# A decoder layer on one core: the last 128 tokens' post norm and residual by VectorE, with no part of it by GpSimd

## The chip, the cores and the metric

The kernel runs on one core of a Trainium2 chip. The metric is the device time of one execution, in microseconds (us); lower is better. The engines are called as in the profile: PE is TensorE's matmul and PEld its weight load, DVE is VectorE, ACT is ScalarE, POOL is GpSimd, SP is SyncE. A name with a q at its end (SPq, POOLq) is the queue of that engine, where DMAs are issued and semaphores are waited for.

## What is computed

One layer of a hybrid decoder trunk on 512 tokens of 1024 channels in float32. A half-step SwiGLU feed-forward network with 2816 hidden channels comes first, then a token mixer (a gated linear recurrence beside sliding-window attention), then a second half-step feed-forward network. Each sub-layer has an RMS norm on its input and another on its output ahead of the residual addition:

```python
def rms_norm(x, g):
    xf = x.astype(jnp.float32)
    y = xf * lax.rsqrt(jnp.mean(xf * xf, axis=-1, keepdims=True) + RMS_EPS)
    return (y * g.astype(jnp.float32)).astype(x.dtype)

def swiglu(x, w_gu, w_down):
    gate, up = jnp.split(x @ w_gu, 2, axis=-1)
    return (jax.nn.silu(gate) * up) @ w_down

x = x + 0.5 * rms_norm(swiglu(rms_norm(x, ffn1_pre_g[l]), ffn1_w_gu[l], ffn1_w_down[l]), ffn1_post_g[l])
...
x = x + rms_norm(y, mix_post_g[l])
x = x + 0.5 * rms_norm(swiglu(rms_norm(x, ffn2_pre_g[l]), ffn2_w_gu[l], ffn2_w_down[l]), ffn2_post_g[l])
```

The change concerns the very last line, and of it the last 128 tokens: the norm of the second network's output `y`, its gain `ffn2_post_g`, and the addition of `x`.

## The kernel before

Nearly all the time goes into matmuls, and float32 products are made of three matmuls each: both operands are split into a high part (rounded) and a low part (the rest), and high times high, high times low and low times high are summed in PSUM. Up to the end, the activations lie transposed, with channels over the 128 partitions and tokens along the free dimension. The kernel goes through the first network, the mixer and the second network in that order. ScalarE rounds the weights to their high parts and VectorE makes the low parts, some steps ahead of the matmuls that use them. The order of the instructions on each engine is the order in which the program writes them; each engine works through its own in order, and waits on semaphores for the others.

The end of the second network makes the output with tokens over the partitions, so that a row of the output can be stored as it is. It goes through the tokens in four blocks of 128, `tb` from 0 to 3. For each block, `ybl` banks in PSUM collect the last hidden channels' part of the down projection (`mm3_out`, lines 1532 to 1534), and the parts of earlier hidden channels lie summed up in the SBUF tiles `yp_b` (in the code `parts[tb, dh]`, with `dh` the left or right 512 output channels). The last block is cut into three pieces, `pieces`: piece 0 is the left 512 columns, piece 1 the next 256, piece 2 the last 256. The earlier blocks have two pieces of 512. Between pieces 0 and 1 of the last block, TensorE transposes the residual `xT` into two PSUM banks, `otp` (in the code `tp`, line 1635).

When the matmuls of a piece are finished:

- line 1642: VectorE adds the PSUM bank to `yp_b`, or subtracts `yp_b` from it (the right half was summed with the other sign).
- line 1643: ScalarE squares the piece, with the sum over the columns going to a column of `ss` by an accumulator that is read at the end.
- line 1649: GpSimd multiplies the piece by the gain, `grow`, in place. It has to wait for the square, which reads the same columns. In the last block's piece 2 it is VectorE (line 1647) that does this, and it writes to another tile, `last`, so that it needn't wait for the square.

When all pieces of a block are through, VectorE adds up the sums of squares (lines 1645 and 1651 for the last block, 1653 for the others), ScalarE takes the root (line 1656), VectorE the reciprocal (line 1657), which gives the scale `rs` of each token. Then VectorE multiplies each piece by `rs` and adds the residual from `otp` in one operation (line 1665), and SyncE issues the store of the piece (line 1666). The last block's piece 1 goes another way: ScalarE has copied the residual's columns from PSUM to the SBUF tile `tail` beforehand (line 1638), scales the piece by `rs` (line 1662), GpSimd adds `tail` (line 1663), and ScalarE's queue issues the store.

After the last instruction, the program closes on line 1691: SyncE waits for all stores, each engine drains, and all report to GpSimd.

Of the kernel before, what the change touches and what calls it, by code (L numbers as in the profile page):

```python
# [11 lines left out]
AF = mybir.ActivationFunctionType  # L12
ALU = mybir.AluOpType
# [3 lines left out]
T = 512  # L17
# [99 lines left out]
def tile_layer(ctx: ExitStack, tc: tile.TileContext, out: bass.AP, **ins: bass.AP):  # L117
    nc = tc.nc
    pe, dve, act, pool, sync = nc.tensor, nc.vector, nc.scalar, nc.gpsimd, nc.sync
# [15 lines left out]
    def bank(name):  # L135
        return psum.tile([P, T], F32, tag="bank", name=name)

    def t2k(name, dt=F32):
        return big.tile([P, T], dt, tag="t2k", name=name, bufs=NT2K)

    def wt(name, w=T, dt=F32):
        return tmp.tile([P, w], dt, tag="w", name=name, bufs=NW)
# [1139 lines left out]
    scale = HD ** -0.5  # L1282
# [210 lines left out]
    for c in range(EARLY):  # L1493
# [9 lines left out]
        if c == EARLY - 2:  # L1503
            bcs = [l.spread() for l in lrms]
            for ci in range(KC):
                for h in range(2):
                    dve.tensor_mul(hl[ci][:, HALF[h]], hl[ci][:, HALF[h]], bcs[h])
                y = t2k(f"ylh{ci}", F32R), t2k(f"yll{ci}", F32R)
# [20 lines left out]
    def mm3_out(ps, h, tb, w, k, cs, start, stop):  # L1529
        (hh, hl_), (hi, lo) = h, w  # L1530
        blk = slice(tb * P, (tb + 1) * P)
        pe.matmul(ps, hh[:, blk], hi[:, k, cs], start=start, stop=False)  # L1532
        pe.matmul(ps, hh[:, blk], lo[:, k, cs], start=False, stop=False)  # L1533
        pe.matmul(ps, hl_[:, blk], hi[:, k, cs], start=False, stop=stop)  # L1534
# [69 lines left out]
    grow = [t2k(f"grow{dh}") for dh in range(2)]  # L1604
# [6 lines left out]
    def weights(f, dh):  # L1611
        k = f - f % 2, dh
        if k not in wd:
            assert order[len(wd)] == k
            wd[k] = W.take(min(3, len(order) - 1 - len(wd)))
        return wd[k]

    for tb in range(NB):
        end = tb == NB - 1
        pieces = [(0, 0, T)] + ([(1, 0, T // 2), (1, T // 2, T)] if end else [(1, 0, T)])  # L1620
        banks = [bank(f"ybl{tb}{i}") for i in range(len(pieces))]
        steps = [(i, f) for i in range(len(pieces)) for f in range(f0, f1)]
        if tb == 0:
            steps = [(i, f) for fs in (range(f0, f0 + 4), range(f0 + 4, f1)) for i in range(2) for f in fs]
        ss = small.tile([P, 3], F32, tag="ss3", name=f"ss_b{tb}")
        tot = small.tile([P, 1], F32, tag="tot", name=f"tot_b{tb}")
        for i, f in steps:
            dh, c0, c1 = pieces[i]
            if (i, f) == (1, f1 - 1 if tb == 0 else f0):

                tp = []
                for h in range(2):
                    tp.append(bank(f"otp{tb}{h}"))
                    for c in range(4):
                        pe.transpose(tp[h][:, c * P:(c + 1) * P], xT[4 * h + c][:, tb * P:(tb + 1) * P], ident)
                if end:
                    tail = wt("tail")[:, :T // 2]
                    act.copy(tail, tp[1][:, :T // 2])
            mm3_out(banks[i][:, :c1 - c0], hs[f - f0], tb, weights(f, dh), f % 2, slice(c0, c1), f == f0, f == f1 - 1)
            if f == f1 - 1:  # L1640
                y = parts[tb, dh][:, c0:c1]
                (dve.tensor_sub if dh else dve.tensor_add)(y, banks[i][:, :c1 - c0], y)  # L1642
                act.activation(wt(f"ysq{tb}{i}")[:, :c1 - c0], y, AF.Square, accum_out=ss[:, i:i + 1])  # L1643
                if end and i == 2:
                    dve.tensor_add(tot, ss[:, 0:1], ss[:, 1:2])
                    last = wt("last")[:, :c1 - c0]
                    dve.tensor_mul(last, y, grow[dh][:, c0:c1])
                else:
                    pool.tensor_mul(y, y, grow[dh][:, c0:c1])  # L1649
        if end:  # L1650
            dve.tensor_add(tot, tot, ss[:, 2:3])
        else:
            dve.tensor_add(tot, ss[:, 0:1], ss[:, 1:2])

        rs = small.tile([P, 1], F32, tag="rs1", name=f"rs_b{tb}")
        act.activation(rs, tot, AF.Sqrt, bias=eps4, scale=4.0 / D)
        dve.reciprocal(rs, rs)
        for i, (dh, c0, c1) in enumerate(pieces):
            y = parts[tb, dh][:, c0:c1]
            if end and i == 1:  # L1660

                act.activation(y, y, AF.Copy, scale=rs)
                pool.tensor_add(y, y, tail)
            else:
                dve.scalar_tensor_tensor(y, last if end and i == 2 else y, rs, tp[dh][:, c0:c1], op0=ALU.mult, op1=ALU.add)
            (act if end and i == 1 else sync).dma_start(out[0, tb * P:(tb + 1) * P, dh * T + c0:dh * T + c1], y)


# [26 lines left out]
```

## Time and profile before

| what | value |
|---|---|
| time, median of 3 runs | 879.47 us (879.43 to 879.74) |
| time of the profiled execution | 880.96 us |
| span of the profiled execution | 879.2 us |
| granted TensorE clock, mean | 0.994 |
| PE busy | 866.2 us (99%), 5732 instructions |
| DVE busy | 680.0 us (77%), 982 instructions |
| ACT busy | 491.3 us (56%), 839 instructions |
| POOL busy | 176.0 us (20%), 179 instructions |

The span runs from the first instruction to the last of one execution that the profiler recorded; its own time is 1.8 us longer than its span and 1.5 us longer than the median of the runs that were timed without a profile. Busy times are sums over the whole span and say little about the last ten microseconds, where TensorE has nothing left to do.

### The profile page before, as it was taken

To read this page: it belongs to the slowest core of one execution; us is meant where nothing else is said; L and a number is where in the kernel's file an instruction comes from. 1 tells how busy PE (TensorE), PEld (TensorE's weight loads), DVE (VectorE), ACT (ScalarE), POOL (GpSimd) and SP (SyncE) were. 2 spreads that over 40 slices of the span, in tenths; PEclk is the share of its full clock that TensorE was granted. 3 is DMA by queue.
4 is the path that set the end of the run, shared out by engine and by line. 5 is a ranking of instruction groups with operands and counts; after the bars stand their busy time and mean duration, and the time that the engine had idled before them with its cause. 6 is when DMAs were issued, how large, how long until landed. Compare 5 with 4: busy or idle time off the path is not lost.

```text
span 879.2 us, 14431 instructions
## 1 busy us (share of the span) xinstructions
PE 866.2 (99%) x5732; PEld 795.2 (90%) x5732; DVE 680.0 (77%) x982; ACT 491.3 (56%) x839; POOL 176.0 (20%) x179
## 2 busy tenths in 40 slices
PE   9999999999999999999999999999999999999995
PEld 8988999989989998998787899888998998998995
DVE  4979758768678864889999589678788789888744
ACT  6647534544435554466787456445556657567542
POOL 2010000000000014444465055211102303205213
PEclk9999999999999999999999999999999999999998
DMA  7242343242243243321311140226573947839901
GB/s 241 74 148 84 103 127 114 73 133 84 73 143 97 84 148 116 97 84 62 109 36 48 49 144 2 96 74 201 188 255 104 229 125 166 196 97 243 279 26 73
DMA packets 91556, 106.10 MB, mean 121 GB/s; under 512 B 4752, under 2 KB 76768, under 8 KB 90976
## 3 DMA queue, kind: packets, MB, share of 16 engines
q1 hardware_dynamic: 83408, 85.64, 30.8%
q0 software_dynamic: 7936, 19.41, 9.5%
q8 instruction: 45, 0.74, 0.3%
q14 instruction: 23, 0.19, 0.1%
q10 hardware_dynamic: 144, 0.13, 0.0%
HBM read 87.86 MB, written 17.30 MB: 120 GB/s over the span
## 4 chain that ended last, share of the span: by engine, by line
PE 91%; DVE 5%; ACT 1%; issue 1%; DMA 1%; POOL 0%; SPq 0%; POOLq 0%; DVEq 0%; ACTq 0%
PE aa L772 12%; PE ab L772 10%; PE da L772 6%; PE db L772 5%; PE ya L408 4%; PE ya L406 4%; PE ya L407 4%; PE ba L772 3%; PE bb L772 3%; PE a_first L948 2%; PE yb L1533 1%; PE yb L1532 1%; PE yb L1534 1%; PE ya L1549 1%; PE ya L1550 1%; PE ya L1551 1%
## 5 line engine op out<-in xcount | busy, mean ns | idle before, releaser
L1558 POOL DMA_DIRECT2D yp_b<-stage x42 | 36.5, 1146 | 147.2 <-ACT stage L1556 138.1
L406 PE MATMUL ya<-hha,whi_ad 128*128 128x512 f32 x158 | 61.5, 389 | 0.0
L407 PE MATMUL ya<-hla,whi_ad 128*128 128x512 f32 x158 | 61.5, 389 | 0.0
L408 PE MATMUL ya<-hha,wlo_ad 128*128 128x512 f32 x158 | 61.5, 389 | 0.0
L1049 POOL MEMSET bd_w_rg<- 128x512 f32 x1 | 0.5, 527 | 266.0 <-PE aa L772 266.0
L408 PEld LDWEIGHTS ya<-hha,wlo_ad 128*128 128x128 f32 x158 | 29.7, 188 | 6.2
L407 PEld LDWEIGHTS ya<-hla,whi_ad 128*128 128x128 f32 x158 | 29.7, 188 | 6.1
L406 PEld LDWEIGHTS ya<-hha,whi_ad 128*128 128x128 f32 x158 | 29.7, 188 | 6.0
L1107 DVE TENSOR_TENSOR yp_a<-ya,yp_a 128x512 f32<-128x512 f32 x24 | 16.4, 686 | 8.8 <-PE ya L408 8.8
L1532 PE MATMUL yb<-whi_bd,hhb 128*128 128x512 f32 x48 | 18.7, 389 | 0.0
L1533 PE MATMUL yb<-wlo_bd,hhb 128*128 128x512 f32 x48 | 18.7, 389 | 0.0
L1534 PE MATMUL yb<-whi_bd,hlb 128*128 128x512 f32 x48 | 18.7, 389 | 0.0
L578 POOL TENSOR_TENSOR acca_r<-acca_r,sq_r 128x512 f32<-128x512 f32 x6 | 8.4, 1406 | 48.1 <-ACT sq_r L437 48.1
L183 DVE TENSOR_TENSOR wlo_bd<-raw_bd,whi_bd 128x1024 fp32r<-128x1024 f32 x10 | 12.1, 1222 | 7.0 <-ACT whi_bd L178 7.0
L1649 POOL TENSOR_TENSOR yp_b<-yp_b,grow 128x512 f32<-128x512 f32 (+1 forms) x8 | 9.7, 1219 | 32.7 <-ACT ysq L1643 32.7
L425 PE MATMUL an<-xh_mx,whi_xl 128*128 128x256 f32 x64 | 15.9, 289 | 0.0
L426 PE MATMUL an<-xh_mx,wlo_xl 128*128 128x256 f32 x64 | 15.5, 283 | 0.0
L705 POOL TENSOR_TENSOR usb<-usb,gsb 128x512 f32<-128x512 f32 x5 | 7.6, 1537 | 33.0 <-DVE usb L702 21.8
L406 PE MATMUL gt<-xh_mx,whi_gt 128*128 128x512 f32 x32 | 14.2, 443 | 0.0
L1643 ACT ACTIVATE ysq<-yp_b 128x512 f32<-128x512 f32 (+1 forms) x9 | 5.2, 583 | 15.1 <-DVE yp_b L1642 14.6
L1532 PE MATMUL ybl<-whi_bd,hhb 128*128 128x512 f32 (+1 forms) x36 | 13.5, 375 | 0.0
L1533 PE MATMUL ybl<-wlo_bd,hhb 128*128 128x512 f32 (+1 forms) x36 | 13.2, 366 | 0.0
(1726 smaller groups left out, 3654.8 us busy)
## 6 DMA issues: line engine op xcount, KB each, us to landing
yp_b<-stage POOLq DMA_DIRECT2D x50, 256.0 KB, 8.2
raw_bd<-in_ffn_w_down SPq DMA_DIRECT2D x4, 1024.0 KB, 8.0
xn<-in_x SPq DMA_DIRECT2D x8, 256.0 KB, 5.2
raw_q<-in_w_in SPq DMA_DIRECT2D x4, 512.0 KB, 3.7
xT_hbm<-xT POOLq DMA_DIRECT2D x2, 1024.0 KB, 11.4
yp_b<-yp_b POOLq DMA_DIRECT2D x8, 256.0 KB, 4.3
xT<-xT_hbm POOLq DMA_DIRECT2D x2, 1024.0 KB, 8.1
out_dram<-yp_b SPq DMA_DIRECT2D x7, 256.0 KB, 2.9
```

What stands on the lines that cost most here:

```text
L406: pe.matmul(ps, hi[:, k, :], xh, start=start, stop=False)
L407: pe.matmul(ps, hi[:, k, :], xl, start=False, stop=False)
L408: pe.matmul(ps, lo[:, k, :], xh, start=False, stop=stop)
L425: pe.matmul(ps[:, sl], hi[:, k, :], xh, start=k == 0, stop=False)
L426: pe.matmul(ps[:, sl], lo[:, k, :], xh, start=False, stop=False)
L772: pe.matmul(o, w[:, k, js], x, start=first and i + j + k == 0, stop=k == 3 and i == 2, skip_group_check=True)
L948: pe.matmul(banks[j][:, HALF[0]], ws[j][part][:, k, :], n1.xs[k][xpart][:, HALF[0]], start=k == 0 and part == xpart, stop=stop and k == KD ...
L1107: dve.tensor_add(parts[c], b, parts[c])
L1532: pe.matmul(ps, hh[:, blk], hi[:, k, cs], start=start, stop=False)
L1533: pe.matmul(ps, hh[:, blk], lo[:, k, cs], start=False, stop=False)
L1534: pe.matmul(ps, hl_[:, blk], hi[:, k, cs], start=False, stop=stop)
L1558: pool.dma_start(parts[2 * tb + i, dh], st, accum_op=ALU.add)
```

## The change

In the last block, all multiplications by the gain are done by VectorE in place, the copy `tail` and the tile `last` are gone, and piece 1 is scaled and added by the same VectorE operation as the other two, with the residual read from PSUM. Its store stays on ScalarE's queue. The first three blocks are as they were. In the built program, the last block's VectorE instructions stand in this order: subtraction or addition of piece 0, multiplication of piece 0, subtraction of piece 1, multiplication of piece 1, subtraction of piece 2, sum of two squares, multiplication of piece 2, sum with the third, reciprocal, and three scalings with addition. GpSimd's last operation is the multiplication of the third block's right half. TensorE's instructions are the same, and so are all that stand before this block on the other engines.

```diff
@@ -1633,9 +1633,6 @@
                     tp.append(bank(f"otp{tb}{h}"))
                     for c in range(4):
                         pe.transpose(tp[h][:, c * P:(c + 1) * P], xT[4 * h + c][:, tb * P:(tb + 1) * P], ident)
-                if end:
-                    tail = wt("tail")[:, :T // 2]
-                    act.copy(tail, tp[1][:, :T // 2])
             mm3_out(banks[i][:, :c1 - c0], hs[f - f0], tb, weights(f, dh), f % 2, slice(c0, c1), f == f0, f == f1 - 1)
             if f == f1 - 1:
                 y = parts[tb, dh][:, c0:c1]
@@ -1643,10 +1640,7 @@
                 act.activation(wt(f"ysq{tb}{i}")[:, :c1 - c0], y, AF.Square, accum_out=ss[:, i:i + 1])
                 if end and i == 2:
                     dve.tensor_add(tot, ss[:, 0:1], ss[:, 1:2])
-                    last = wt("last")[:, :c1 - c0]
-                    dve.tensor_mul(last, y, grow[dh][:, c0:c1])
-                else:
-                    pool.tensor_mul(y, y, grow[dh][:, c0:c1])
+                (dve if end else pool).tensor_mul(y, y, grow[dh][:, c0:c1])
         if end:
             dve.tensor_add(tot, tot, ss[:, 2:3])
         else:
@@ -1657,12 +1651,7 @@
         dve.reciprocal(rs, rs)
         for i, (dh, c0, c1) in enumerate(pieces):
             y = parts[tb, dh][:, c0:c1]
-            if end and i == 1:
-
-                act.activation(y, y, AF.Copy, scale=rs)
-                pool.tensor_add(y, y, tail)
-            else:
-                dve.scalar_tensor_tensor(y, last if end and i == 2 else y, rs, tp[dh][:, c0:c1], op0=ALU.mult, op1=ALU.add)
+            dve.scalar_tensor_tensor(y, y, rs, tp[dh][:, c0:c1], op0=ALU.mult, op1=ALU.add)
             (act if end and i == 1 else sync).dma_start(out[0, tb * P:(tb + 1) * P, dh * T + c0:dh * T + c1], y)
```

## The prediction, as it was made ahead of the run

> **What bounds the kernel now.** I read the page first, then the chain that ended last over the final 15 us, then the timeline of each engine there, then the closing instructions (line 1691).
>
> ```profile
> span 879.2 us, 14431 instructions
> PE 91%; DVE 5%; ACT 1%; issue 1%; DMA 1%; POOL 0%; SPq 0%; POOLq 0%; DVEq 0%; ACTq 0%
> ```
>
> TensorE holds 91% of the chain, and the change touches none of its instructions. Only what follows TensorE's last matmul can move.
>
> ```profile
> 869.74 0.28 PE L1534 MATMUL ybl<-whi_bd,hlb 128*128 128x256 f32 x1
> ```
>
> TensorE is done at 870.02, so 9.2 us of the 879.2 are the tail. The end of the chain (start, length, what):
>
> ```profile
> 865.17 1.29 POOL yp_b L1649
> ...
> 868.75 1.98 POOL yp_b L1649 x2
> 870.74 1.71 issue
> 872.44 0.76 POOLq L1691
> ```
>
> The chain ends in GpSimd's queue, on line 1691, which is where the program closes: each engine drains, reports, and GpSimd collects the reports. The chain follows it only to 873.2, when GpSimd's last addition is done. The closing instructions that start before 878 (count, shortest/median/longest in ns, first and last start) show the rest:
>
> ```profile
> L1691 SPq EVENT_SEMAPHORE  x9: 28/28/28, 873.5 to 875.5; - x9
> L1691 SPq DRAIN  x2: 7/7/7, 875.6 to 875.7; - x2
> L1691 PEldq DRAIN  x1: 2345/2345/2345, 867.7 to 867.7; - x1
> L1691 DVEq DRAIN  x1: 1122/1122/1122, 872.0 to 872.0; - x1
> L1691 POOLq DRAIN  x1: 5991/5991/5991, 872.4 to 872.4; - x1
> L1691 ACTq DRAIN  x1: 148/148/148, 873.6 to 873.6; - x1
> ```
>
> SyncE waits for the stores one after another and is through at 875.7. TensorE's drain ends at 870.1, VectorE's at 873.1, ScalarE's at 873.8. GpSimd's begins at 872.44 and lasts 5.99 us, to 878.43. Only then does GpSimd take its first semaphore:
>
> ```profile
> L1691 POOLq EVENT_SEMAPHORE  x4: 17/17/17, 878.5 to 879.1; - x4
> ```
>
> So the last arrival is GpSimd's drain and not the stores: 2.8 us pass between SyncE's 875.7 and GpSimd's 878.5, and the closing takes the remaining 0.7 us to 879.2. That is the wait to argue about. The work that feeds it, VectorE, then ScalarE, GpSimd and SyncE (start, length, line, operation, idle time before it):
>
> ```profile
> 867.24 0.68 DVE L1642 TENSOR_TENSOR yp_b<-ybl,yp_b 128x512 f32<-128x512 f32 x1
> 868.62 0.42 DVE L1642 TENSOR_TENSOR yp_b<-ybl,yp_b 128x256 f32<-128x256 f32 x1 [0.70 <-PE ybl L1534]
> 870.06 0.42 DVE L1642 TENSOR_TENSOR yp_b<-ybl,yp_b 128x256 f32<-128x256 f32 x1 [1.01 <-PE ybl L1534]
> 870.40 0.35 DVE L1645 TENSOR_TENSOR tot_b<-ss_b 128x1 f32<-128x1 f32 x1
> 870.67 0.41 DVE L1647 TENSOR_TENSOR last<-yp_b,grow 128x256 f32<-128x256 f32 x1
> 871.12 0.16 DVE L1651 TENSOR_TENSOR tot_b<-tot_b,ss_b 128x1 f32<-128x1 f32 x1
> 871.90 0.75 DVE L1665 SCALAR_TENSOR_TENSOR yp_b<-yp_b,rs_b,otp 128x512 f32<-128x512 f32 x1
> 872.57 0.47 DVE L1665 SCALAR_TENSOR_TENSOR yp_b<-last,rs_b,otp 128x256 f32<-128x256 f32 x1
> ```
>
> ```profile
> 867.96 0.63 ACT L1643 ACTIVATE ysq<-yp_b 128x512 f32<-128x512 f32 x1 [2.34 <-DVE yp_b L1642]
> 868.49 0.18 ACT L1643 ACTIVATION_READ_ACCUMULATOR ysq<-yp_b 128x1 f32 x1
> 868.59 0.35 ACT L1638 COPY tail<-otp 128x256 f32<-128x256 f32 x1
> 869.42 0.42 ACT L1643 ACTIVATE ysq<-yp_b 128x256 f32<-128x256 f32 x1 [0.48 <-ACT tail L1638]
> 869.75 0.19 ACT L1643 ACTIVATION_READ_ACCUMULATOR ysq<-yp_b 128x1 f32 x1
> 870.57 0.42 ACT L1643 ACTIVATE ysq<-yp_b 128x256 f32<-128x256 f32 x1 [0.64 <-DVE yp_b L1642]
> 870.90 0.19 ACT L1643 ACTIVATION_READ_ACCUMULATOR ysq<-yp_b 128x1 f32 x1
> 871.89 0.51 ACT L1662 ACTIVATE yp_b<-yp_b,rs_b 128x256 f32<-128x256 f32 x1 [0.29 <-DVE rs_b L1657]
> 873.24 0.37 ACTq L1666 DMA_DIRECT2D out_dram<-yp_b  x1
> ```
>
> ```profile
> 872.48 0.73 POOL L1663 TENSOR_TENSOR yp_b<-yp_b,tail 128x256 f32<-128x256 f32 x1 [1.74 <-ACT yp_b L1662]
> ```
>
> ```profile
> 872.68 0.81 SPq L1666 DMA_DIRECT2D out_dram<-yp_b  x2
> ```
>
> **The change, part by part.** *Removed from GpSimd:* its last three operations, two multiplications (1.98 us) and the closing addition (0.73 us). Its last operation becomes the multiplication of the block before, 865.17 to 866.46, so its drain is reached 7.3 us sooner. Two bounds for when it ends then: with the lag that VectorE's drain has behind VectorE's last operation (873.10 against 873.04) it is 866.5; with the lag that GpSimd's has now (878.43 against 873.21, 5.2 us) it is 871.7. Either way it is hidden by the stores, by 4 us or more, so which one holds does not matter. The 2.8 us go. What is late next is SyncE's report that the stores have landed.
>
> *Added to VectorE:* three multiplications written in place, where one wrote to another tile, and one scaling-and-addition of 256 columns. An in-place multiplication must wait until ScalarE has squared the same columns, and VectorE runs in order, so behind each waiting multiplication stands the subtraction that feeds ScalarE's next square. An operation on 512 columns with both operands in SBUF takes 684 ns, by this row:
>
> ```profile
> L785 DVE TENSOR_TENSOR g1b<-g1b,u4b 128x512 f32<-128x512 f32 x8 | 5.5, 684 | 0.3 <-ACT g1b L806 0.3
> ```
>
> One of 256 takes 0.41 (line 1647). An operation with nothing to wait for starts 0.08 before its forerunner ends (872.57 against 872.65), and one that waits for ScalarE starts 0.03 after it (871.12 against 871.09). Step by step:
>
> 1. Piece 0's square is read at 868.67, as now. Its multiplication runs from 868.70 to 869.38.
> 2. Piece 1's subtraction starts at 869.30 instead of 868.62 and ends at 869.72.
> 3. Piece 1's square follows 0.09 later, as piece 2's does now (870.48 to 870.57), at 869.81: the copy that delays it now (0.48 idle, by its row) is gone. Square and read take 0.52, to 870.33.
> 4. Piece 1's multiplication runs from 870.36 to 870.77; piece 2's subtraction starts at 870.69 instead of 870.06. TensorE has long finished.
> 5. Piece 2's square starts 0.51 after the subtraction does and takes 0.52, to 871.72. Its multiplication starts at 871.75, and the sum of the squares at 872.08 instead of 871.12: 0.96 later.
> 6. From that sum to the first scaling-and-addition it is 0.78, as now: 872.86. The second starts 0.67 later, at 873.53, the third 0.39 later, at 873.92, and ends at 874.39.
> 7. The stores: piece 0 at 873.64 instead of 872.68 (+0.96); piece 1 from ScalarE's queue at 874.03; piece 2 from SyncE's at 874.42, last, where piece 1's at 873.24 is last now (+1.18).
>
> *Removed from ScalarE:* the copy (0.35 us) and the scaling (0.51 us); step 3 uses the one, and the other leaves the path with the addition. ScalarE's queue then holds only its store, which waits for VectorE.
>
> *The stores* are the same three, 256, 128 and 128 KB on the same queues. If moving the 512 KB limits, the landing shifts with the first issue, by 0.96; if the last issue limits, by 1.18. I take 1.1, nearer to the last issue, since the issues now spread over 0.8 us instead of 0.56.
>
> **The sum.** 2.8 us of waiting for the drain go, and 1.1 us come on the store path: -1.7 us, between -1.84 and -1.62. The profiled execution took 880.96 us, 1.8 over its span, and 1.5 over the median of the runs; I expect the same distances, so it becomes 879.3 with a span of 877.5. On the median, 879.47 - 1.7 = 877.8 us.
>
> The short sum of squares on line 1645 took 0.35 us while GpSimd was multiplying (to 870.73), the same operation on line 1651 took 0.16 with GpSimd idle. That 0.19 goes, but the sum then lies under the square of step 5, so by these rows it is worth nothing. The Trainium skill, "Perfetto Trace Analysis", section "Optimizing Scalar/DVE Operations", says that GpSimd and VectorE share a read port to SBUF, so that moving work between the two may bring nothing. The trace agrees that they hinder each other; by the rule, GpSimd's multiplications cost VectorE time already and the move would cost up to those 0.19 us less than step 7 has, a sum of -1.9.
>
> **Rivals.** *The drain is not GpSimd's own work* (slower). Its 5.99 us could wait on what the whole tail does, or be long only in a profiled execution. The place is the same drain. If its end keeps its distance to the last store's issue (878.43 against 873.24), it moves by 1.18 to 879.6. If it isn't there in a timed run, both kernels end with their stores and the store path's 1.1 is all that is left. Either way +1.2, 880.7; it decides as soon as the new drain ends after about 876.8. For it: the other engines' drains end within 0.2 us of their last work, GpSimd's 5.2 us after, and nothing in the trace says why. Against it: no other engine's work lies between 873.8 and 875.4, so an engine that waited for the others would have had nothing to wait for beyond 875.7. A longer ScalarE lag in steps 3 and 5 could carry it past +1.76. I give it 17%. The Trainium skill, "VectorE: DVE Perf Modes", section "The DRAIN you can't avoid", says that the drains before and after a kernel are a constant of about 12 ns on all five engines: by that rule GpSimd's drain would be no price of GpSimd's work, which is this rival. The trace disagrees for this drain, with its 5991 ns.
>
> *A store lands late.* The earlier stores of 256 KB took longer from issue to landing than the last ones:
>
> ```profile
> out_dram<-yp_b SPq DMA_DIRECT2D x7, 256.0 KB, 2.9
> ```
>
> The last store now needs 2.2 us (873.24 to the semaphores that SyncE takes up to 875.5). At 2.9 it adds 0.7: -1.0, 878.5 us. Against: none of the three last stores did so. 9%.
>
> *The change does not do what it says* is excluded: in the built order GpSimd's last operation is the multiplication of the block before, and VectorE's tail has the operations of steps 1 to 6 in that order.
>
> **How the numbers follow.** A measurement of this kernel can tell about 0.2%, 1.76 us, from no change. The forecast (74%) lies at -1.7, just inside; with 0.2 us of error in the steps it falls on either side of that line, so 35% go to faster and 39% to the same. The slower rival gives 10% to the same and 7% to slower, the late store 9% to the same. Faster 0.35, same 0.58, slower 0.07. The forecast's own range is 877.2 to 878.3; to keep 8 in 10 with the two rivals, it reaches up to 880.7.
>
> **What would show it.** Right: GpSimd's drain starts near 865.2 and ends before SyncE's last wait; the chain ends with a store's landing, with no idle time before GpSimd's first closing semaphore other than SyncE's; the sum of squares starts near 872.1 and VectorE ends near 874.4. Wrong: GpSimd's drain still ends last, or the last store is issued before 874 or after 874.8.

## The result, and the profile after

The changed kernel takes 877.46 us, the median of 10 runs (876.76 to 877.91). The kernel before, run beside it, takes 879.55 us (10 runs, 878.92 to 881.13). The ratio is 0.9974, with a 95% interval of 0.9964 to 0.9984: 2.1 us less, clear of no change, and beyond the prediction's line of 0.2% by its middle but not by the whole of the interval. The profiled execution took 877.85 us. Of the experiments below, one of e2's 11 runs took 2223 us, with TensorE slow throughout, and the times of e4 lie in two groups some 2 us apart, so e2 is read from the profile of e5, the same kernel once more, and e4 from its tail.

```profile
span 876.1 us, 14426 instructions
```

The span is 3.1 us shorter than before's 879.2, but 1.05 us of that has nothing to do with the change, as TensorE's last matmul shows (start, length):

```profile
868.69 0.28 PE L1534 MATMUL ybl<-whi_bd,hlb 128*128 128x256 f32 x1
```

It ends at 868.97, against 870.02 before, although TensorE's instructions are the same, and in e1 below, which has the whole change in it, it ends at 870.02 again. The granted clock was 0.998 in this execution and 0.994 in that of before; that this alone makes the 1.05 is not shown. So the two kernels are compared by their tails, from the end of the last matmul to the end of the span: 9.2 us before, 7.15 after, 2.05 less, which is what the timed runs say too. To compare a moment of this trace with one of before, add 1.05. The closing, now on line 1680, without its last 0.7 us (count, shortest/median/longest in ns, first and last start):

```profile
L1680 SPq EVENT_SEMAPHORE  x10: 17/28/28, 873.7 to 875.2; - x10
L1680 SPq DRAIN  x2: 7/10/13, 875.3 to 875.4; - x2
L1680 POOLq DRAIN  x1: 6556/6556/6556, 864.1 to 864.1; - x1
L1680 PEldq DRAIN  x1: 2345/2345/2345, 866.7 to 866.7; - x1
L1680 DVEq DRAIN  x1: 1570/1570/1570, 871.8 to 871.8; - x1
L1680 ACTq DRAIN  x1: 147/147/147, 873.3 to 873.3; - x1
L1680 POOLq EVENT_SEMAPHORE  x1: 17/17/17, 875.4 to 875.4; - x1
```

GpSimd's drain now starts at 864.09 and ends 6.56 us later, at 870.64. That is 4.7 us before SyncE is through with the stores, at 875.37, and GpSimd takes its first semaphore at once, at 875.39. The 2.8 us between SyncE and GpSimd are gone. The drain itself did not get shorter. GpSimd's last operation is now the one ahead of the last block:

```profile
864.12 1.29 POOL L1643 TENSOR_TENSOR yp_b<-yp_b,grow 128x512 f32<-128x512 f32 x1 [1.40 <-ACT ysq L1640]
```

It ends at 865.42, and the drain ends 5.23 us behind it. Before, the last operation ended at 873.21 and the drain at 878.43, also 5.23 us behind. This lag is what the experiments follow. VectorE's tail, then ScalarE's (start, length, line, operation, idle time before it):

```profile
867.67 0.69 DVE L1643 TENSOR_TENSOR yp_b<-yp_b,grow 128x512 f32<-128x512 f32 x1 [0.79 <-ACT ysq L1640]
868.27 0.42 DVE L1639 TENSOR_TENSOR yp_b<-ybl,yp_b 128x256 f32<-128x256 f32 x1
869.32 0.42 DVE L1643 TENSOR_TENSOR yp_b<-yp_b,grow 128x256 f32<-128x256 f32 x1 [0.62 <-ACT ysq L1640]
869.66 0.42 DVE L1639 TENSOR_TENSOR yp_b<-ybl,yp_b 128x256 f32<-128x256 f32 x1
869.99 0.15 DVE L1642 TENSOR_TENSOR tot_b<-ss_b 128x1 f32<-128x1 f32 x1
870.71 0.43 DVE L1643 TENSOR_TENSOR yp_b<-yp_b,grow 128x256 f32<-128x256 f32 x1 [0.57 <-ACT ysq L1640]
871.05 0.15 DVE L1645 TENSOR_TENSOR tot_b<-tot_b,ss_b 128x1 f32<-128x1 f32 x1
871.76 1.53 DVE L1654 SCALAR_TENSOR_TENSOR yp_b<-yp_b,rs_b,otp 128x512 f32<-128x512 f32 x3
```

```profile
868.77 0.42 ACT L1640 ACTIVATE ysq<-yp_b 128x256 f32<-128x256 f32 x1 [1.14 <-issue]
870.17 0.42 ACT L1640 ACTIVATE ysq<-yp_b 128x256 f32<-128x256 f32 x1 [0.89 <-DVE tot_b L1642]
872.94 0.37 ACTq L1655 DMA_DIRECT2D out_dram<-yp_b  x1
```

Each multiplication waits for ScalarE's square of the same columns (0.79, 0.62 and 0.57 us idle), and the subtraction of the next piece stands behind it. The chain that ended last now runs through this tail. The view follows it only to VectorE's last operation; the landing of the stores and SyncE's waits come after it. Before, it ended in GpSimd's queue:

```profile
871.76 0.75 DVE yp_b L1654
872.51 0.39 DVEq L1680
872.90 0.39 DVE yp_b L1654
```

### The profile page after: what moved, and what is told of

Same layout as the page of the kernel before. It is cut to its first block, busy times and chain, and to the rows that moved or that the text cites. A ratio compares the mean times of both kernels' runs of the same rounds, so it can differ in the third digit from the quotient of the medians.

```text
span 876.1 us, 14426 instructions
## 1 busy us (share of the span) xinstructions
PE 864.9 (99%) x5732; PEld 793.9 (91%) x5732; DVE 681.5 (78%) x985; ACT 490.5 (56%) x837; POOL 172.9 (20%) x176
## 5 line engine op out<-in xcount | busy, mean ns | idle before, releaser
L1643 POOL TENSOR_TENSOR yp_b<-yp_b,grow 128x512 f32<-128x512 f32 x6 | 7.7, 1288 | 30.4 <-ACT ysq L1640 30.4
```

## The experiments

**The theory and its rival.** The theory is the prediction's: the drain follows GpSimd's own last operation by a fixed lag, so the program ends with the drain or with the stores, whichever is later. The rival is that the end of the drain follows what the whole tail does, or the stores, and that it came earlier in the changed kernel for another reason than GpSimd's own last operation. The layer's kernels are compared by the tail and by the lag:

| kernel | last matmul ends | GpSimd's last operation ends | drain ends | lag | SyncE through | span ends | tail |
|---|---|---|---|---|---|---|---|
| before | 870.02 | 873.21 | 878.43 | 5.23 | 875.68 | 879.23 | 9.2 |
| after | 868.97 | 865.42 | 870.64 | 5.23 | 875.37 | 876.14 | 7.15 |
| e1 | 870.02 | 873.05 | 878.28 | 5.23 | 876.41 | 879.07 | 9.06 |
| e5 | 868.21 | 872.61 | 877.84 | 5.23 | 875.07 | 878.63 | 10.42 |
| e3 | 868.67 | 865.12 | 870.34 | 5.23 | 874.09 | 874.86 | 6.19 |
| e4 | 870.40 | 871.12 | 876.34 | 5.23 | 875.87 | 877.14 | 6.74 |
| g3 | 868.23 | 871.41 | 875.98 | 4.57 | 873.89 | 876.77 | 8.54 |
| g4 | 868.14 | 864.59 | 869.82 | 5.23 | 874.54 | 875.31 | 7.16 |

**e1: one tiny operation on GpSimd, late.** The changed kernel, and a 128x1 product that nobody reads:

```diff
         dve.reciprocal(rs, rs)
+        if end:
+            z = small.tile([P, 1], F32, tag="z", name="z")
+            pool.tensor_mul(z, rs, rs)
```

> The changed kernel, with one GpSimd multiplication of 128x1 added after the reciprocal, whose result nobody reads. The tail (from the end of TensorE's last matmul to the end of the span) is 9.2 us before the change and 7.1 after it. Theory (GpSimd's drain ends 5.2 us after GpSimd's last operation, whatever its size): the operation ends about 3.0 us into the tail, the drain at 8.2, the tail is 8.9 to 9.0, and the time is 1.8 us above the changed kernel's, about 879.3. Rival (the drain grows with the work that GpSimd did, or waits on the other engines): the tail stays at 7.1 to 7.3 and the time at 877.5.

Measured: 879.59 us, median of 11 runs; the ratio to before is 1.0004 (0.9995 to 1.0013).

```profile
872.86 0.19 POOL L1654 TENSOR_TENSOR z<-rs_b 128x1 f32<-128x1 f32 x1 [6.39 <-DVE rs_b L1651]
L1683 POOLq DRAIN  x1: 5457/5457/5457, 872.8 to 872.8; - x1
L1683 SPq DRAIN  x2: 7/7/7, 876.3 to 876.4; - x2
```

One operation of 0.19 us gives the whole gain back. The drain ends at 878.28, 1.9 us after SyncE is through. VectorE, ScalarE and the stores are those of the changed kernel (SyncE is through 6.39 us after the last matmul, there 6.40), so it is GpSimd's own last operation, however small, that sets the drain.

**e2 and e5: the in-place multiplications alone.** The kernel before, with the three multiplications by VectorE in place; the copy, ScalarE's scaling and GpSimd's closing addition stay:

```diff
-                    last = wt("last")[:, :c1 - c0]
-                    dve.tensor_mul(last, y, grow[dh][:, c0:c1])
-                else:
-                    pool.tensor_mul(y, y, grow[dh][:, c0:c1])
+                (dve if end else pool).tensor_mul(y, y, grow[dh][:, c0:c1])
...
-                dve.scalar_tensor_tensor(y, last if end and i == 2 else y, rs, tp[dh][:, c0:c1], op0=ALU.mult, op1=ALU.add)
+                dve.scalar_tensor_tensor(y, y, rs, tp[dh][:, c0:c1], op0=ALU.mult, op1=ALU.add)
```

> The kernel before, with the three multiplications of the last block by VectorE in place, as the change has them; the copy, ScalarE's scaling and GpSimd's closing addition stay. Theory (the end is GpSimd's last operation plus 5.2 us plus 0.7, and VectorE's waits for the squares put that operation off by 0.96): the tail grows from 9.2 to 10.2 us and the time by 1.0, to 880.5. Rival (the drain's end does not follow GpSimd's last operation): the stores have 2.8 us of room, so the tail stays at 9.2 and the time at 879.5.

Measured: 880.82 us, median of 11 runs, ratio 1.0015 (1.0006 to 1.0024). The profile is that of e5, the same kernel once more:

> The same kernel as in e2 (the kernel before with the in-place multiplications by VectorE), once more, for a profile that can be laid beside the others. Theory (GpSimd's closing addition 0.96 us later, drain 5.2 us after it): the addition ends 4.1 to 4.2 us after TensorE's last matmul, where it is 3.2 before the change, and the tail is 10.1 to 10.2 us. Rival (the drain does not follow the addition): tail 9.2 us.

Measured: 880.36 us in one run (before beside it 879.87), and a tail of 10.42 us.

```profile
867.93 0.28 PE L1534 MATMUL ybl<-whi_bd,hlb 128*128 128x256 f32 x1
871.89 0.72 POOL L1660 TENSOR_TENSOR yp_b<-yp_b,tail 128x256 f32<-128x256 f32 x1 [7.23 <-ACT yp_b L1659]
L1688 POOLq DRAIN  x1: 5984/5984/5984, 871.9 to 871.9; - x1
```

GpSimd's addition ends 4.40 us after the last matmul, against 3.19 before, and the drain moves with it, 1.2 us. That is 0.2 to 0.3 us more than was expected, for the addition and for the tail. The copy on line 1638 is still there, and with it ScalarE starts the square of piece 1 0.37 us after the subtraction ends (868.31 against 867.94), where it is 0.08 in the changed kernel, which has no copy (868.77 against 868.69). Two of GpSimd's three tail operations are gone here, and nothing is gained. By itself that part of the change is a loss: it is GpSimd's last operation that counts, and the in-place multiplications on VectorE make that one later.

**e3: the waits of the in-place multiplications.** The changed kernel, with the products in tiles of their own, so that they needn't wait for the squares:

```diff
-                (dve if end else pool).tensor_mul(y, y, grow[dh][:, c0:c1])
+                if end:
+                    yg.append(wt(f"yg{i}")[:, :c1 - c0])
+                    dve.tensor_mul(yg[i], y, grow[dh][:, c0:c1])
+                else:
+                    pool.tensor_mul(y, y, grow[dh][:, c0:c1])
...
-            dve.scalar_tensor_tensor(y, y, rs, tp[dh][:, c0:c1], op0=ALU.mult, op1=ALU.add)
+            dve.scalar_tensor_tensor(y, yg[i] if end else y, rs, tp[dh][:, c0:c1], op0=ALU.mult, op1=ALU.add)
```

> The changed kernel, with the three multiplications written to tiles of their own, so that none waits for a square. Theory (the in-place waits cost VectorE 0.96 us on the path to the last store, and nothing but the stores sets the end): subtractions start as soon as TensorE is done, as in the kernel before, the last store is issued 0.9 us earlier than in the changed kernel, the tail is 6.2 to 6.3 us, the time 876.6. Rival (the stores' landing, not VectorE, sets the end, or the in-place waits were hidden): the tail stays at 7.0 to 7.1 and the time at 877.5.

Measured: 876.43 us, median of 5 runs (876.26 to 876.57), ratio to before 0.9962 (0.9950 to 0.9975); a tail of 6.19 us.

```profile
868.71 0.42 DVE L1640 TENSOR_TENSOR yp_b<-ybl,yp_b 128x256 f32<-128x256 f32 x1 [0.55 <-PE ybl L1534]
869.17 0.43 DVE L1646 TENSOR_TENSOR yg<-yp_b,grow 128x256 f32<-128x256 f32 x1
869.77 0.16 DVE L1650 TENSOR_TENSOR tot_b<-tot_b,ss_b 128x1 f32<-128x1 f32 x1 [0.17 <-ACT ysq L1641]
```

Piece 2's subtraction waits for TensorE again and not for ScalarE, and the last sum of squares starts 1.10 us after the last matmul, where it is 2.08 in the changed kernel: the in-place waits cost 0.98 us, and with them gone the drain, at 870.34, is still hidden. Of the versions run, this is the fastest, ahead of both kernels.

**e4: GpSimd keeps its multiplications, but not the addition.** The kernel before, without the copy and with piece 1 scaled and added by VectorE:

```diff
-                if end:
-                    tail = wt("tail")[:, :T // 2]
-                    act.copy(tail, tp[1][:, :T // 2])
...
-            if end and i == 1:
-
-                act.activation(y, y, AF.Copy, scale=rs)
-                pool.tensor_add(y, y, tail)
-            else:
-                dve.scalar_tensor_tensor(y, last if end and i == 2 else y, rs, tp[dh][:, c0:c1], op0=ALU.mult, op1=ALU.add)
+            dve.scalar_tensor_tensor(y, last if end and i == 2 else y, rs, tp[dh][:, c0:c1], op0=ALU.mult, op1=ALU.add)
```

> The kernel before without the middle piece's way over ScalarE and GpSimd: GpSimd multiplies pieces 0 and 1 as before, VectorE multiplies piece 2 to a tile of its own and does all three scalings with addition. Theory (drain 5.2 us after GpSimd's last operation, which ends 0.7 us into the tail): the drain ends at 5.9 to 6.0, the stores are through at 5.5, the tail is 6.7 and the time 2.5 us below the kernel before, about 877.0, 0.4 above the kernel with the multiplications out of place on VectorE. Rival (what was gained by the change is VectorE's multiplications, not the drain): the time is no better than the changed kernel's 877.5 or stays near 879.5.

Measured: a tail of 6.74 us, as expected; 878.46 us, median of 11 runs (876.63 to 879.49), ratio 0.9975 (0.9967 to 0.9984). The median is 1.2 us below that of the kernel before, where 2.5 were expected, and by itself it would not exclude the rival. The trace does: the drain ends 5.94 us after the last matmul and the stores are through at 5.47, both where the theory had them.

```profile
869.14 1.98 POOL L1646 TENSOR_TENSOR yp_b<-yp_b,grow 128x512 f32<-128x512 f32 x2 [2.29 <-ACT ysq L1640]
L1683 POOLq DRAIN  x3: 51/98/6281, 870.1 to 876.9; - x3
L1683 SPq DRAIN  x3: 7/7/7, 875.8 to 876.6; - x3
L1683 POOLq EVENT_SEMAPHORE  x4: 17/17/17, 876.4 to 877.0; - x4
```

The drain still ends last, at 876.34, but only 0.47 us after SyncE. Taking piece 1's way over ScalarE and GpSimd out, with GpSimd's closing addition at its end, was worth 2.5 us of tail by itself (9.2 to 6.74). That is more than the whole change brings (7.15), which moves the multiplications as well.

**What the lag is made of.** Six kernels look at it. Five are small ones without the layer: they load x in 128x1024 tiles, square each, and store the squares. In f1 the loads are SyncE's and the squares GpSimd's; the others change who does what:

```diff
 not f1:  -        sync.dma_start(x, ins["x"][0, tb * P:(tb + 1) * P, :])
 f2, f3:  +        pool.dma_start(x, ins["x"][0, tb * P:(tb + 1) * P, :])
 f3 only: -        pool.tensor_mul(y, xs[tb], xs[tb])
          +        nc.vector.tensor_mul(y, xs[tb], xs[tb])
 g1:      +        for q in range(0, P, 32):
          +            pool.dma_start(x[q:q + 32, :], ins["x"][0, tb * P + q:tb * P + q + 32, :])
 g2:      +        for c in range(0, D, 256):
          +            pool.dma_start(x[:, c:c + 256], ins["x"][0, tb * P:(tb + 1) * P, c:c + 256])
```

f1, four squares and no DMA on GpSimd:

> A small kernel that leaves out the whole layer: SyncE loads x in four tiles, GpSimd squares each in place of everything else, SyncE stores the squares. GpSimd issues no DMA. If the 5.2 us between GpSimd's last operation and the end of its drain come from its arithmetic alone, the drain ends 5.2 us after the last multiplication. If they come from the DMAs that GpSimd issues in the layer, the drain ends within 0.2 us of it.

f2, the same with four loads issued by GpSimd:

> The same small kernel (x squared, the layer left out), but GpSimd issues the four loads itself, ahead of its multiplications. If the arithmetic alone makes the 5.2 us, the drain ends 5.2 us after the last multiplication as without these DMAs; if the DMAs do, 5.2 us here and under 0.2 without them; if each adds something, more than without them.

f3, four loads by GpSimd and the squares by VectorE:

> The same small kernel (x squared, the layer left out), with the four loads issued by GpSimd and the multiplications done by VectorE, so that GpSimd does no arithmetic. If the arithmetic makes the 5.2 us, GpSimd's drain ends within 0.5 us of its last DMA issue; if the DMAs do, some 5 us after it.

Measured: 17.22, 17.95 and 18.51 us, one run each. GpSimd's last squares and its drains in f1, then in f2 (the first of the three drains is the long one):

```profile
8.24 3.74 POOL L44 TENSOR_TENSOR y<-x 128x1024 f32<-128x1024 f32 x2 [0.37 <-DMA x<-in_x]
L70 POOLq DRAIN  x3: 34/76/2524, 9.5 to 15.2; - x3
```

```profile
8.95 3.74 POOL L44 TENSOR_TENSOR y<-x 128x1024 f32<-128x1024 f32 x2 [0.22 <-DMA x<-in_x]
L70 POOLq DRAIN  x3: 34/95/2831, 10.3 to 15.9; - x3
```

Without DMAs of its own, GpSimd's drain ends 0.07 us after its last operation (12.05 against 11.98). With four it ends 0.41 after (13.10 against 12.69), though all four had landed, since the squares read them. In f3 GpSimd does nothing but issue:

```profile
1.24 2.22 POOL L40 DMA_DIRECT2D x<-in_x  x4 [0.80 <-PEq L70]
L70 POOLq DRAIN  x3: 34/95/8519, 2.6 to 16.5; - x3
```

The last issue ends at 3.47 and the drain at 11.08, 7.6 us later. The last packet of the loads ends at 10.57, their landing is complete at 10.87, and the drain ends 0.2 us after that. So in this one run the drain ends as one would that also waits for GpSimd's own DMAs to land; how that adds up with the 0.41 us of f2 is not shown. What it needs besides, for DMAs that are long done, grows with something about them. g1 and g2 ask what, with 16 DMAs:

> The small kernel (x squared, the layer left out) with GpSimd's loads cut into 16 DMAs of 32 rows instead of 4 of 128, the same bytes in the same packets. With 4 such DMAs GpSimd's drain ended 0.41 us after its last multiplication, with none 0.07, and in the layer, with 63, it is 5.23. If each DMA that GpSimd issued costs its drain 0.08 to 0.09 us, the lag is 1.35 to 1.45 here. If each packet does, it stays at 0.4. If the lag does not depend on them, it stays at 0.4 as well.

> The small kernel (x squared, the layer left out) with GpSimd's loads cut into 16 DMAs of 128 rows and 256 columns, four times the packets of a quarter of the size. A cost of 0.08 to 0.09 us for each DMA gives a lag of 1.35 to 1.45 us, the same as with 16 DMAs of 32 rows; a cost for each packet gives about 1.4 as well, four times that of the same bytes in few packets; a cost for the bytes gives 0.4.

Measured: 21.95 and 22.67 us. g1, then g2:

```profile
9.23 7.44 POOL L45 TENSOR_TENSOR y<-x 128x1024 f32<-128x1024 f32 x4
L71 POOLq DRAIN  x3: 45/95/5507, 12.5 to 19.9; - x3
```

```profile
9.96 7.43 POOL L45 TENSOR_TENSOR y<-x 128x1024 f32<-128x1024 f32 x4
L71 POOLq DRAIN  x3: 39/95/6417, 12.4 to 20.6; - x3
```

The lags are 1.38 and 1.39 us. g1 moves the same bytes as f2 in the same 512 packets of data, with four times as many DMAs, and (1.38 - 0.07) / 16 = 0.082 us for each is close to what f2 had, (0.41 - 0.07) / 4 = 0.085. So the cost goes with the DMAs, and not with the data or its packets. Each DMA also brings 16 packets of under 512 B (64 in f2, 256 in g1), and a cost for each of these can't be told here from a cost for each DMA. g2 was to have had four times the packets of data; its records show 512 as well, so it separates nothing further.

**g3: fewer GpSimd DMAs in the layer.** The layer's GpSimd issues 63 DMAs, 42 of them on line 1558. The kernel before, with eight stores, which it issues 245 us and more before GpSimd's drain starts, issued by ScalarE instead:

```diff
-                pool.dma_start(parts[tb, dh], st)
+                act.dma_start(parts[tb, dh], st)
```

> The kernel before, with the eight stores of line 1590 (early in the second network's down projection) issued by ScalarE instead of GpSimd, so that GpSimd issues 55 DMAs and not 63. If its drain pays 0.08 us for each DMA issued in the whole program, the drain ends 4.55 to 4.6 us after the closing addition instead of 5.23, the tail is 8.5 to 8.6 us instead of 9.2, and the time 0.6 below the kernel before. If the lag is a constant of the layer, it stays at 5.23 and the time at 879.5.

Measured: a lag of 4.57 us, a tail of 8.54; 878.74 us, median of 10 runs (before 879.58), ratio 0.9995 (0.9985 to 1.0004), so the times alone don't tell it from no change.

```profile
870.69 0.72 POOL L1663 TENSOR_TENSOR yp_b<-yp_b,tail 128x256 f32<-128x256 f32 x1 [1.74 <-ACT yp_b L1662]
L1691 POOLq DRAIN  x3: 51/93/5331, 870.6 to 876.5; - x3
```

The tail's work is that of before, and the lag is 0.66 us shorter for 8 DMAs less, 0.082 each. With f1's 0.07 the layer's lag is 0.07 + 63 x 0.082 = 5.2 us, which is the 5.23 of every other layer. Why a DMA costs this at the end is not shown.

**g4: the queues of the last two stores swapped.** The changed kernel, for the one number that the prediction had wrong, below:

```diff
-            (act if end and i == 1 else sync).dma_start(out[0, tb * P:(tb + 1) * P, dh * T + c0:dh * T + c1], y)
+            (act if end and i == 2 else sync).dma_start(out[0, tb * P:(tb + 1) * P, dh * T + c0:dh * T + c1], y)
```

> The changed kernel with the last two stores' queues exchanged: SyncE issues piece 1 behind piece 0, ScalarE issues piece 2, the last. In the kernel before, the last store (ScalarE's) landed 2.2 us after its issue, in the changed kernel the last one (SyncE's) 1.9. If that is because the three issues are spread over 0.8 us instead of 0.56, the last one lands 1.9 us after its issue here too and the tail stays at 7.1. If ScalarE's queue is the slower one, it lands 2.2 after and the tail is 7.3 to 7.4.

Measured: 877.03 us in one run, and a tail of 7.16 us, that of the changed kernel. The last store, now ScalarE's, is issued at 872.50 and lands at 874.39, 1.89 us later.

```profile
872.50 0.37 ACTq L1655 DMA_DIRECT2D out_dram<-yp_b  x1
L1680 SPq DRAIN  x3: 7/7/7, 874.5 to 874.8; - x3
```

## Why the prediction was right

The mechanism held, step by step. The sum was -1.7 us and the timed runs say -2.1, inside the forecast's own range (877.2 to 878.3). The forecast lay just short of the 0.2% line and the measured medians just beyond it. The prediction had left the side open (35% for faster, 39% for the same), and what carried the result over is the mis-sized term below.

- **The drain goes.** It was to start near 865.2 and end before SyncE's last wait; with the 1.05 added it starts at 865.14. Of the two bounds for its end, the one with GpSimd's present lag is the right one: 871.7 was worked out, 870.64 + 1.05 = 871.7 measured. As said, it does not matter, with the stores 4.7 us later. The whole 2.8 us went. Of the signs that the prediction named, one can't be read off as it was put: the view's chain ends on VectorE's last operation and not on a landing. That the landing comes last shows in SyncE's closing semaphores, the last of them at 875.23, just after the last store's 875.22.
- **Steps 1 to 6.** With 1.05 added, the sum of squares starts at 872.10 (872.08 worked out), the first scaling at 872.81 (872.86), and VectorE ends at 874.35 (874.39). The in-place waits cost what the order of the squares said, and e3 shows them by themselves, at 0.98 us.
- **Step 7.** The stores are issued at 873.59, 873.99 and 874.37, each 0.04 to 0.05 before the times worked out.
- **The term that was mis-sized** is the landing. It was taken to shift by 1.1 us with the issues; SyncE is through 6.40 us after the last matmul, before 5.66, so the store path took 0.74 more. The last issue did move by 1.13, but that store lands 1.89 us after its issue, where before it was 2.17, and SyncE is through 0.15 after the landing instead of 0.27. (Before, SyncE still has three semaphores to take after that landing, from 875.42 to 875.55, since it asks for ScalarE's store first; now it is one.) So the sum is -2.8 + 0.74 = -2.06, and the tails differ by 2.05. Of the cause, g4 excludes the queue that issues the last store: on ScalarE's it lands in 1.89 too. What is left is the spread of the issues, 0.8 us instead of 0.56. The traces fit it: in before, e5 and g3, with 0.56, the last store lands 2.16 to 2.18 us after its issue, and in the changed kernel, e1, e3, e4 and g4, with 0.78 to 0.79, 1.88 to 1.89. Before, the last store is issued only 0.13 us after the second and still lands 0.30 after it. The spread was not tried by itself.
- **The shared port.** The first sum of squares took 0.15 us instead of 0.35, with GpSimd idle, and so it is in all the layer's kernels of the table: 0.35 or 0.36 in before, e4 and g3, where GpSimd is multiplying, 0.15 in the changed kernel, e1, e3, e5 and g4, where it is idle. So GpSimd does hinder VectorE, as the Trainium skill has it in "Perfetto Trace Analysis", section "Optimizing Scalar/DVE Operations"; that the port which they share is the reason is not shown here. It was worth nothing on the path, as the prediction said: the next sum starts where step 5 put it.
- **The rival of the drain that isn't GpSimd's own** falls by e1, e4 and e5, where the drain follows GpSimd's last operation by 5.23 us wherever that lies, and it is in the timed runs too: e1's are as slow as before's. With it falls, for this drain, the rule in the Trainium skill's "VectorE: DVE Perf Modes", section "The DRAIN you can't avoid", of some 12 ns on every engine; the runs show 0.07 us and 0.08 more for each DMA that GpSimd issued.
- **The late store** did not occur; the landing was shorter, not longer.

What the prediction could not say is why the drain is long. It did not need it for its sum, but with it the rival would have had less than its 17%.

## What to carry to other kernels

At the end of a program, look at each engine's closing drain beside SyncE's last wait for the stores: the later one is the end, and the last operation of an engine whose drain ends long after it costs that lag, however small it is. On GpSimd count the DMAs that it issued and, by these runs, give its last operation that many times 0.08 us ahead of the last store's landing. An in-place operation that follows another engine's read of the same columns puts that read into its own engine's order; where a tile is free, write to it instead.

## What the runs showed of the hardware

GpSimd's closing drain costs about 0.08 us for each DMA that GpSimd has issued in the whole program: lags of 0.07, 0.41, 1.38, 1.39, 4.57 and 5.23 us for 0, 4, 16, 16, 55 and 63 DMAs. It is counted from GpSimd's last operation even where the last of these DMAs was issued 37 us before the drain starts (at 826.7, line 1602, in the changed kernel). In the one run where some were still under way (f3), the drain ended 0.2 us after the last of them had landed.
